# The last two gate columns of a hybrid encoder layer: two plain products, or a fourth seven-product unit

## The chip, the cores and the metric

The kernel runs on one core of a Trainium2 chip. The metric is the device time of one execution in microseconds (us), and for a kernel the median of its runs. A profile is one further execution that the hardware profiler recorded. Engines are named as the profile names them: PE is the matrix engine (PEld its weight loads), DVE the vector engine, ACT the scalar engine, POOL the GpSimd engine, SP the sync engine, which here only issues transfers. POOL issues transfers too, on a queue of its own.

## What is computed

One encoder layer over 1024 prompt frames and 32 sample frames, 1056 tokens in all. The part that matters here is the input product `z = h @ W_in`, whose last 2048 columns are the gates of the two branches:

```python
h = _rms_norm(x, g_pre_mix)
z = h @ w_in
qa, ka, va, qb, fb, ib, ob, ga, gb = jnp.split(z, SPLIT_POINTS, axis=-1)
...
mix = jax.nn.sigmoid(ga) * (ya @ w_br_a) + jax.nn.sigmoid(gb) * (yb @ w_br_b)
x = x + _rms_norm(mix @ w_out, g_post_mix)
```

`ya` comes from windowed attention, `yb` from a gated linear recurrence of eight heads. The kernel cuts the 2048 gate columns into 16 gate columns of 128, eight for `ga` and eight for `gb`, and writes for each the tanh of half the logit to memory.

## The kernel before

Activations lie transposed: 128 partitions of the model dimension by tokens, in three groups of 384, 384 and 288 tokens. `La[g]` and `Lb[g]` hold the high and low part of group g, eight slices of the model dimension each. A product of precision float32 is three matmuls: high weight by high part, high weight by low part, low weight by high part. A plain gate column takes, for each group, 8 slices times 3 matmuls.

The kernel runs in stages: attention with its input products (to about 356 us of the span), the recurrence with its input products (to about 826 us), the tail of gate columns that is the matter of this change (826 to 852 us), the branch products `ya @ w_br_a` and `yb @ w_br_b` (from 852 us, matmuls into `st` tiles from operand pages `oa` and weights `wt`), then the output product and the feed-forward part.

In the recurrence stage the input columns are computed in units of two columns by `unit_pieces`. A unit takes the first two token groups and the two columns as a 2 by 2 block product and needs seven block products in place of eight (a Winograd form of Strassen's scheme); each is a piece of 4 slices times 3 matmuls of 384 tokens. The block sums of the activations stand ready in `SX`: numbers 0, 2 and 7 are halves of `La`/`Lb`, numbers 1, 3, 4 and 6 are the sums in `TH0` to `TH3` with low parts `TL0` to `TL3`. The third group, of 288 tokens, takes four plain pieces of 12 matmuls out of `GX`. A unit's weights are made by `b_parts`: DVE forms four sums, and each of eight parts of 128 x 512 gets a cast on ACT (its high part, L1043) and a subtraction on DVE (its low part, L1044). The results stand in PSUM banks X, Y, Z and G; the evacuations e0 to e10 read them on ACT and DVE, and a gate column then has its tanh on ACT (L299) and its store on SP.

The heads' units come in order (q and f, then i and og); after heads 3 and 7 follows a unit of two gate columns. `unit_at` and `BU` list them. `b_raw` puts a unit's raw weights in the buffers `wr` (2) or `wb` (8) by turns, counted from the last unit. The recurrence's small steps (`tile_in`, `tile_out`, `group_out`) are hung on the pieces by number with `at`. What is left of head 7 after its last unit is hung on the tail.

The tail before is `u` and `v`, the last two gate columns as plain products of three blocks each, 24 matmuls a block. Since the recurrence uses the space of `La[1][0:4]` and `Lb[1][0:4]` for its gate tile, `back` reloads them from memory (`h_d`, eight transfers of 192 KB). The first three blocks run with the recurrence's steps, the last three with the preparation of the branch stage: POOL loads the operand pages (`a_load`, L1557: two of each product number, called (0,0) to (6,1) below), and `a_split` makes high and low parts of them, a cast on ACT (L1564) and a subtraction on DVE (L1565). The branch weights come through SP (`wa`, L1533) and are split at L228 and L229. The tile framework orders each engine's instructions by itself, after the program's order and its guess at durations.

Of the kernel before, what the change touches and what calls it, by code (L numbers as in the profile page):

```python
# [10 lines left out]
F32 = mybir.dt.float32  # L11
F32R = mybir.dt.float32r
# [47 lines left out]
def layer_kernel(  # L60
# [17 lines left out]
    def nm(s):  # L78
        n_names[0] += 1
        return f"{s}_{n_names[0]}"  # L80
# [67 lines left out]
    def in_cols(c):  # L148
        return rows_cols(w_in, 0, c, P, KT)
# [12 lines left out]
            plan.append(in_cols(b[1] * P if b[0] == "q" else GATES[b[1]][1]))  # L162
    plan.append(in_cols(GATES[N_A][1]))
    n_first = len(plan)
    plan += [in_cols(c) for _, c in GATES[14:]]
    n_gates = len(plan)
    plan += [rows_cols(w_out, 0, c * P, P, KT) for c in (*range(8), *range(8))]
    n_mix = len(plan)
    limit = [n_first]
# [7 lines left out]
    def load_next():  # L177
        _, kt, n = plan[len(ready)]
        if len(raws) == len(ready):
            load_raw()  # L180
        raw = raws[len(ready)]
        hi = wp.tile([P, kt, n], F32R, tag="wb", name=nm("wh"), bufs=8)
        lo = wp.tile([P, kt, n], F32R, tag="wb", name=nm("wl"), bufs=8)
        S.copy(hi[:], raw[:])
        if lo_by[0] == "vector":
            V.tensor_tensor(lo[:], raw[:], hi[:].bitcast(F32), op=ALU.subtract)
        else:
            S.mul(lo[:], raw[:], -1.0)
            gdma(lo[:], raw[:], accum_op=ALU.add)
        ready.append((hi, lo))  # L190
# [89 lines left out]
    def unit(out):  # L280

        cell = []

        def get_w():
            if not cell:
                cell.append(next_w())
            return cell[0]
        return [(get_w, g, out) for g in range(3)]
# [6 lines left out]
    def gate_out(dst):  # L295
        def out(g, b):
            o, n = GR[g]
            t = gtile()
            S.activation(t[:, :n], b[:, :n], AF.Tanh, scale=0.5)  # L299
            dma(dst[:, o:o + n], t[:, :n])  # L300
        return out
# [698 lines left out]
    def rows4(t):  # L1000
        return [t[:, k, :] for k in range(4)]
# [15 lines left out]
    for h in range(8):  # L1017
        unit_at[h] = len(BU)
        BU += [(1280 + h * P, 2304 + h * P), (3328 + h * P, 4352 + h * P)]
        if h in G_AFTER:  # L1020
            BU.append(tuple(GATES[G_AFTER[h] + a][1] for a in range(2)))
    NB = len(BU)
    raw_b, ready_b, gens_b, n_b = {}, [], {}, [0]

# [65 lines left out]
    with right("bp") as bp:  # L1090
        def bt(tag, cols, bufs, dt=F32):
            return bp.tile([P, cols], dt, tag=tag, name=nm(tag), bufs=bufs)
# [11 lines left out]
        HD = [{} for _ in range(8)]  # L1104
        ahead_b = 3

        def unit_pieces(u, f1_dest, f1, f2_dest, f2):

            c = {}

            def piece(t, seq, x, n, first):
                def run():
                    if first and t not in c:
                        c[t] = bank(pb, t, 1)
                    b_prepare(min(8 * u + seq + ahead_b, 8 * NB - 1))
                    w = ready_b[8 * u + seq]
                    o = c[t][:, :n]
                    for k in range(4):  # L1120
                        wh, wl = w[:, 0, k, :], w[:, 1, k, :]
                        E.matmul(o, wh, x[0][k], start=first and k == 0, stop=False,  # L1122
                                 skip_group_check=True)
                        E.matmul(o, wh, x[1][k], start=False, stop=False, skip_group_check=True)
                        E.matmul(o, wl, x[0][k], start=False, stop=k == 3, skip_group_check=True)
                return run

            def st(t, seq, first=False):
                return piece(t, seq, SX[seq], 384, first)

            def cl(t, seq, first=False):
                return piece(t, seq, GX[seq], 288, first)

            def b(t, n=384):
                return c[t][:, :n]

            def e0():
                c["s1c"] = bt("s1c", GMAX, 1)
                S.copy(c["s1c"][:], b("X"))

            def e2():
                c["U2"] = f1_dest()
                V.tensor_tensor(c["U2"], c["s1c"][:], b("Y"), op=ALU.subtract)

            def e5():
                c["U3"] = f2_dest(1)
                V.tensor_tensor(c["U3"], b("Y"), c["s1c"][:], op=ALU.subtract)

            def e6():
                V.tensor_tensor(c["U3"], c["U3"], b("Z"), op=ALU.subtract)  # L1150
                f2(1, c["U3"])

            def e8():
                d = f2_dest(0)
                V.tensor_tensor(d, b("Y"), c["s1c"][:], op=ALU.subtract)
                f2(0, d)

            def e10():
                V.tensor_tensor(c["U2"], c["U2"], b("Z"), op=ALU.add)
                f1(1, c["U2"])  # L1160

            def g1a():
                c["G"] = bank(pb, "G", 1)
                cl("G", 0, True)()

            def g2a():
                c["G"] = bank(pb, "G", 1)
                cl("G", 5, True)()

            return [(st("X", 0, True), e0), (g1a, None), (st("Y", 1, True), e2),  # L1170
                    (st("X", 2), lambda: f1(0, b("X"))), (cl("G", 2), lambda: f1(2, b("G", 288))),
                    (st("Y", 3), e5), (st("Z", 4, True), e6), (g2a, None), (st("Y", 6), e8),
                    (cl("G", 6), lambda: f2(2, b("G", 288))), (st("Z", 7), e10)]
# [36 lines left out]
            return unit_pieces(unit_at[h] + 1, i_dest, i_out, lambda g: bt("x0", GMAX, 1)[:], og_out)  # L1210

        def gate_unit(h):
            a, b = (gate_out(GATES[G_AFTER[h] + i][0]) for i in range(2))
            return unit_pieces(unit_at[h] + 2, lambda: gu, a,
                               lambda g: bt("x0", GMAX, 1)[:], b)

        def v_turn(h, g):
            d = HD[h]
# [183 lines left out]
        def at(m, f, *a):  # L1402
            small.setdefault(m, []).append(lambda: f(*a))
# [27 lines left out]
            for g, m in enumerate((13, 14, 16) if last else (16, 18, 21)):  # L1431
                at(m1 + m, group_out, h, g)

        def back():

            for part, t in (("La", La), ("Lb", Lb)):
                t[1][0:4] = rows4(lp.tile([P, 4, 384], F32R, tag=f"{part}10", name=nm(part)))
            for part, t in zip(h_d, (La, Lb)):
                for k in range(4):
                    dma(t[1][k].bitcast(F32), part[:, k, :])  # L1440

        def more():
            limit[0] = n_gates
            load_next()

        at(len(pieces) - 1, back)
        at(len(pieces) - 2, more)
        w_sums = [(3, 0, 0, None), (4, 0, 1, None), (1, 0, 0, None), (6, 1, 0, None),
                  (3, 0, 1, None), (4, 1, 1, None), (1, None, None, 4), (6, None, None, 1)]
        def block_sum(dst, src, acc):  # L1450
# [29 lines left out]
        for m, (run, ev) in enumerate(pieces):  # L1480
# [2 lines left out]
                ev()  # L1483
            for f in small.pop(m, ()):
                f()
        u, v = (unit(gate_out(dst)) for dst, _ in GATES[14:])
        tail = [u[0], u[2], v[0], v[2], u[1], v[1]]
        n_bank[0] += 2
        stream(tail[:3], {m - len(pieces): f for m, f in small.items()})
    bctx.close()  # L1490


# [88 lines left out]
        small[m] = [lambda x=x: both(a_prepare, x) if isinstance(x, int) else both(a_split, *x)  # L1581
                    for x in at_m]
    small[3].append(lambda: a_load(2, 1, gdma))
    stream(tail[3:], small)
    lctx.close()
    pctx.close()
    with right("mp") as mp:
# [1368 lines left out]
```

## Time and profile before

| | |
|---|---|
| median of three runs | 1937.41 us (1937.32 to 1943.33) |
| the profiled execution | 1941.95 us |
| its span, from first to last instruction | 1940.2 us |
| matmuls | 14523 |
| busy share of DVE, ACT, POOL | 76%, 53%, 20% |
| moved by DMA | 329 MB, 170 GB/s on average |

The busy shares are means over stages with different limits. In the views below, a window's row gives its start and end, its length, then the busy time of PE, PEld, DVE, ACT and POOL, each with its number of instructions, then the clock that PE was granted, the busy share of the 16 DMA engines and what they moved in GB/s. A row of the timeline gives start, duration, engine, source line, operation, tiles and shape; in square brackets stand the idle time of the engine before it and what ended that.

### The profile page before, as it was taken

To read this page: it belongs to the slowest core of one execution; us is meant where nothing else is said; L and a number is where in the kernel's file an instruction comes from. 1 tells how busy PE (TensorE), PEld (TensorE's weight loads), DVE (VectorE), ACT (ScalarE), POOL (GpSimd) and SP (SyncE) were. 2 spreads that over 40 slices of the span, in tenths; PEclk is the share of its full clock that TensorE was granted. 3 is DMA by queue.
4 is the path that set the end of the run, shared out by engine and by line. 5 is a ranking of instruction groups with operands and counts; after the bars stand their busy time and mean duration, and the time that the engine had idled before them with its cause. 6 is when DMAs were issued, how large, how long until landed. Compare 5 with 4: busy or idle time off the path is not lost.

```text
span 1940.2 us, 38175 instructions
## 1 busy us (share of the span) xinstructions
PE 1919.0 (99%) x14523; PEld 1900.5 (98%) x14523; DVE 1473.5 (76%) x3201; ACT 1028.7 (53%) x2214; POOL 383.8 (20%) x530
## 2 busy tenths in 40 slices
PE   8999999999999999999999999999999999999999
PEld 8999999999999999999999999999999999999998
DVE  6777777788887888756796878778787786768872
ACT  7667777666666666553445763333333336534432
POOL 2111211001101010022321113444644430000000
PEclk9999999999999999999999999999999999999999
DMA  8534443545537464489979784566897357754343
GB/s 267 151 106 134 120 139 84 156 111 142 146 95 155 121 139 101 127 288 308 289 194 298 242 274 126 166 168 186 165 181 190 110 179 235 221 179 155 116 132 87
DMA packets 319599, 329.11 MB, mean 170 GB/s; under 512 B 17432, under 2 KB 277435, under 8 KB 319416
## 3 DMA queue, kind: packets, MB, share of 16 engines
q1 hardware_dynamic: 274152, 218.92, 36.6%
q0 software_dynamic: 45136, 107.70, 23.1%
q8 instruction: 114, 1.87, 0.4%
q14 instruction: 69, 0.57, 0.1%
q10 hardware_dynamic: 128, 0.06, 0.0%
HBM read 234.48 MB, written 132.47 MB: 189 GB/s over the span
## 4 chain that ended last, share of the span: by engine, by line
PE 87%; DVE 5%; DMA 3%; ACT 3%; issue 2%; SPq 0%; POOL 0%; ACTq 0%; DVEq 0%; POOLq 0%
PE st L2377 7%; PE st L2376 7%; PE st L2375 7%; PE mm L207 4%; PE mm L205 4%; PE mm L206 4%; PE st L2505 4%; PE st L2507 4%; PE st L2506 4%; PE st L1667 3%; PE st L1669 3%; PE st L1671 3%; PE st L205 2%; PE st L206 2%; PE st L207 2%; PE Y L1122 2%
## 5 line engine op out<-in xcount | busy, mean ns | idle before, releaser
L2375 PE MATMUL st<-op,wt 128*128 128x264 f32 x1232 | 348.6, 283 | 1.7 <-DVE x L1921 0.8
L2377 PE MATMUL st<-op,wt 128*128 128x264 f32 x1232 | 349.8, 284 | 0.0
L2376 PE MATMUL st<-op,wt 128*128 128x264 f32 x1232 | 347.7, 282 | 0.0
L2375 PEld LDWEIGHTS st<-op,wt 128*128 128x128 f32 x1232 | 231.2, 188 | 3.1 <-issue 1.0
L2376 PEld LDWEIGHTS st<-op,wt 128*128 128x128 f32 x1232 | 231.4, 188 | 0.0
L2377 PEld LDWEIGHTS st<-op,wt 128*128 128x128 f32 x1232 | 230.8, 187 | 0.0
L2505 PE MATMUL st<-dop,wt 128*128 128x264 f32 x616 | 174.5, 284 | 1.0 <-ACT S L2520 0.7
L2507 PE MATMUL st<-dop,wt 128*128 128x264 f32 x616 | 174.3, 283 | 0.0
L2506 PE MATMUL st<-dop,wt 128*128 128x264 f32 x616 | 173.8, 283 | 0.0
L2034 ACT CAST wt<-wu 128x512 fp32r<-128x512 f32 x126 | 76.0, 618 | 176.3 <-POOL wu L2043 71.4
L205 PE MATMUL mm<-La,wh 128*128 128x384 f32 (+1 forms) x480 | 158.2, 330 | 0.0
L206 PE MATMUL mm<-Lb,wh 128*128 128x384 f32 (+1 forms) x480 | 155.4, 324 | 0.5 <-DVE Lb L784 0.4
L207 PE MATMUL mm<-La,wl 128*128 128x384 f32 (+1 forms) x480 | 155.0, 323 | 0.2 <-DVE wl L759 0.2
L2035 DVE TENSOR_TENSOR wt<-wu,wt 128x512 fp32r<-128x512 f32 x126 | 86.5, 695 | 46.0 <-ACT wt L2034 46.0
L2505 PEld LDWEIGHTS st<-dop,wt 128*128 128x128 f32 x616 | 115.6, 188 | 1.7 <-ACT S L2520 1.2
L2506 PEld LDWEIGHTS st<-dop,wt 128*128 128x128 f32 x616 | 115.6, 188 | 0.0
L2507 PEld LDWEIGHTS st<-dop,wt 128*128 128x128 f32 x616 | 115.5, 188 | 0.0
L2139 ACT CAST wt<-wd 128x512 fp32r<-128x512 f32 (+1 forms) x84 | 48.9, 586 | 90.0 <-PE st L2507 70.1
L206 PEld LDWEIGHTS mm<-Lb,wh 128*128 128x128 f32 x480 | 90.4, 189 | 1.7 <-DVE Lb L784 1.4
L207 PEld LDWEIGHTS mm<-La,wl 128*128 128x128 f32 x480 | 90.2, 188 | 0.5 <-DVE wl L759 0.5
L1043 ACT CAST wt<-wu 128x512 fp32r<-128x512 f32 x108 | 65.1, 618 | 47.8 <-DVE wu L1051 23.9
L1122 PE MATMUL G<-La,wt 128*128 128x288 f32 x288 | 90.4, 314 | 0.0
(628 smaller groups left out, 6353.9 us busy)
## 6 DMA issues: line engine op xcount, KB each, us to landing
wu<-in_w_up_dram SPq DMA_DIRECT2D x42, 512.0 KB
wu<-in_w_in_dram SPq DMA_DIRECT2D x36, 512.0 KB
w_d<-in_w_down_dram POOLq DMA_DIRECT2D x24, 704.0 KB, 8.6
a_d<-Up SPq DMA_DIRECT2D x21, 528.0 KB
wr<-in_w_in_dram SPq DMA_DIRECT2D x21, 512.0 KB
s_d<-sm SPq DMA_DIRECT2D x40, 264.0 KB
dop<-s_d SPq DMA_DIRECT2D x16, 528.0 KB
wr<-in_w_out_dram SPq DMA_DIRECT2D x16, 512.0 KB
```

The lines of the kernel that those rows point to most:

```text
L205: E.matmul(ps, wh, a, start=first and n == 0, stop=False)
L206: E.matmul(ps, wh, b, start=False, stop=False)
L207: E.matmul(ps, wl, a, start=False, stop=last and n == len(ks) - 1)
L1122: E.matmul(o, wh, x[0][k], start=first and k == 0, stop=False, skip_group_check=True)
L2034: S.copy(t[:, 0], src)
L2035: V.tensor_tensor(t[:, 1], src, t[:, 0].bitcast(F32), op=ALU.subtract)
L2375: E.matmul(o, wh, xh, start=first and k == 0, stop=False, skip_group_check=True)
L2376: E.matmul(o, wh, xl, start=False, stop=False, skip_group_check=True)
L2377: E.matmul(o, wl, xh, start=False, stop=k == 3, skip_group_check=True)
L2505: E.matmul(o, wh, xh_, start=first and k == 0, stop=False, skip_group_check=True)
L2506: E.matmul(o, wh, xl_, start=False, stop=False, skip_group_check=True)
L2507: E.matmul(o, wl, xh_, start=False, stop=k == ng - 1, skip_group_check=True)
```

## The change

The last two gate columns become one more unit, number 18 (`unit_at[8]`), with pieces in an order of their own (`last`). Its first five pieces run with the recurrence's steps, its last six with the preparation of the branch stage. The two plain columns, their weights in the plan and the reload `back` go.

```diff
     n_first = len(plan)
-    plan += [in_cols(c) for _, c in GATES[14:]]
-    n_gates = len(plan)
     plan += [rows_cols(w_out, 0, c * P, P, KT) for c in (*range(8), *range(8))]
...
+    unit_at[8] = len(BU)
+    BU.append(tuple(GATES[14 + a][1] for a in range(2)))
     NB = len(BU)
...
+            def g2x():
+                c["G"] = bank(pb, "X", 1)
+                cl("G", 5, True)()
+
+            if last:
+                return [(st("X", 0, True), e0), (st("Y", 1, True), e2), (st("Y", 3), e5),
+                        (st("Z", 4, True), e6), (st("Y", 6), e8), (st("Z", 7), e10),
+                        (st("X", 2), lambda: f1(0, b("X"))), (g1a, None),
+                        (cl("G", 2), lambda: f1(2, b("G", 288))), (g2x, None),
+                        (cl("G", 6), lambda: f2(2, b("G", 288)))]
...
-        def back():
-
-            for part, t in (("La", La), ("Lb", Lb)):
-                t[1][0:4] = rows4(lp.tile([P, 4, 384], F32R, tag=f"{part}10", name=nm(part)))
-            for part, t in zip(h_d, (La, Lb)):
-                for k in range(4):
-                    dma(t[1][k].bitcast(F32), part[:, k, :])
...
+        tail = gate_unit(8)
+        pieces += tail[:5]
...
-        u, v = (unit(gate_out(dst)) for dst, _ in GATES[14:])
-        tail = [u[0], u[2], v[0], v[2], u[1], v[1]]
-        n_bank[0] += 2
-        stream(tail[:3], {m - len(pieces): f for m, f in small.items()})
+        for m in sorted(small):
+            for f in small[m]:
+                f()
...
-    stream(tail[3:], small)
+    for m, (run, ev) in enumerate(tail[5:]):
+        run()
+        if ev is not None:
+            ev()
+        for f in small.get(m, ()):
+            f()
```

Line numbers of the kernel move by a few. Three places in the order of the instructions are spoken of later.

POOL, at the start of the tail, before: the load of the sample's recurrent state `S`, then the operand pages `oa` in the order (0,0), (1,0), (2,0), (0,1), (1,1), (2,1), (3,0), (3,1), then the first gate tiles `ta`. In brackets stand the engines and queues that a row waits for.

```order
L1321 DMA S_10813<-in_state_hgrn_dram 128x128 [waits DMASW2_49,DMASW5_49,DVE_49,PE_49]
L1557 DMA oa_10934<-ya_d 128x1056
L1557 DMA oa_10933<-sa_d_112 128x1056 [waits DMASW4_49]
L1557 DMA oa_10932<-ya_d 128x1056
L1557 DMA oa_10931<-ya_d 128x1056 [waits DMASW6_49]
L1557 DMA oa_10930<-sa_d_112 128x1056
```

The same place of POOL's order in the changed kernel.

```order
L1331 DMA S_10816<-in_state_hgrn_dram 128x128 [waits DMASW2_49,DMASW5_49,DVE_49,PE_49]
L1554 DMA oa_10938<-ya_d 128x1056 [waits PE_49]
L1554 DMA oa_10937<-sa_d_112 128x1056 [waits DMASW4_49]
L1554 DMA oa_10936<-ya_d 128x1056
L1554 DMA oa_10935<-ya_d 128x1056 [waits DMASW6_49]
L1554 DMA oa_10934<-sa_d_112 128x1056
```

The first page load now waits for PE; the count that it waits for is that of the last matmul of the tail's fifth piece, which reads `TH3`, in whose space the pages lie. All others stand behind it on POOL.

ACT, where the tail hands over to the branch stage, before: tanh of a tail gate (L299), casts of operand pages (L1564) and of branch weights (L228), and the first copy out of an `st` tile (L1675).

```order
L299 ACTIVATE gt_11019<-G_10992 128x384 [waits DMAHW7_49,PE_49,Activation_49]
L1564 CAST oa_10933<-oa_10933 128x1056 [waits DMASW4_49]
L1564 CAST oa_10932<-oa_10932 128x1056 [waits DMASW5_49]
L228 CAST wt_10989<-wa_10956 128x512
L1564 CAST oa_10931<-oa_10931 128x1056 [waits DMASW6_49]
L299 ACTIVATE gt_11059<-X_11028 128x384 [waits DMAHW3_49,PE_49,Activation_49]
L1564 CAST oa_10930<-oa_10930 128x1056 [waits DMASW7_49]
L228 CAST wt_11024<-wa_10956 128x512 [waits DMAHW0_49]
L228 CAST wt_11044<-wa_10986 128x512 [waits DMAHW1_49]
L228 CAST wt_11062<-wa_10986 128x512 [waits DMAHW2_49]
L1675 COPY as_11107<-st_11093 128x264 [waits PE_49]
```

ACT at the same place in the changed kernel.

```order
L297 ACTIVATE gt_11026<-G_10999 128x288 [waits DMAHW0_49,PE_49,Activation_49]
L1561 CAST oa_10937<-oa_10937 128x1056 [waits DMASW4_49]
L1561 CAST oa_10936<-oa_10936 128x1056 [waits DMASW5_49]
L226 CAST wt_10996<-wa_10963 128x512 [waits DMAHW1_49]
L297 ACTIVATE gt_11066<-X_11035 128x288 [waits DMAHW1_49,PE_49,Activation_49]
L1561 CAST oa_10935<-oa_10935 128x1056 [waits DMASW6_49]
L1561 CAST oa_10934<-oa_10934 128x1056 [waits DMASW7_49]
L226 CAST wt_11031<-wa_10963 128x512 [waits DMAHW2_49]
L226 CAST wt_11051<-wa_10993 128x512 [waits DMAHW2_49]
L226 CAST wt_11069<-wa_10993 128x512 [waits DMAHW3_49]
L1677 COPY as_11114<-st_11100 128x264 [waits PE_49]
```

The same eleven rows, from a tail gate's tanh to the first copy; the two tanh are of 288 tokens instead of 384, and the first of them waits for the ninth piece of the tail instead of the fifth block.

DVE, in head 0 of the recurrence, before: from the first factor products to the evacuation e2 (L1143, into `vt`) of the unit i and og.

```order
L1286 TENSOR_TENSOR d_925_5221<-d_925_5221,tf 128x384
L1287 TENSOR_TENSOR ke_5222<-ke_5222,tf 128x384
L1288 COPY dec_5202<-cb 128x3
L1291 SCALAR_TENSOR_TENSOR tq_5058<-tq_5058,cb 128x384
L1044 TENSOR_TENSOR wt_5240<-sa_5115,wt_5240 128x512
L1143 TENSOR_TENSOR vt_5259<-s1c_5200,Y_5239 128x384
```

DVE in the changed kernel, some 15 rows earlier, up to the scans (L1245).

```order
L1044 TENSOR_TENSOR wt_5185<-sa_5115,wt_5185 128x512
L1155 TENSOR_TENSOR tf<-Y_5017,s1c_4998 128x384
L1056 TENSOR_TENSOR wu_5021<-wu_5021 128x512
L1044 TENSOR_TENSOR wt_5240<-sa_5115,wt_5240 128x512
L1159 TENSOR_TENSOR x_907_5037<-x_907_5037,Z_5096 128x384
L1245 SCALAR_TENSOR_TENSOR cb<-resets,cb 128x384 x2
```

With one more unit, the raw weights of units 0 and 1 change buffers; the subtraction for part `wt_5240` now stands ahead of the scans and no longer directly ahead of e2.

More of the change, by code (lines that the diff above doesn't have):

```diff
@@ L1105, in layer_kernel, with unit_pieces @@
         ahead_b = 3
-        def unit_pieces(u, f1_dest, f1, f2_dest, f2):
+        def unit_pieces(u, f1_dest, f1, f2_dest, f2, last=False):
             c = {}
@@ L1212, in gate_unit @@
         def gate_unit(h):
-            a, b = (gate_out(GATES[G_AFTER[h] + i][0]) for i in range(2))
-            return unit_pieces(unit_at[h] + 2, lambda: gu, a,
-                               lambda g: bt("x0", GMAX, 1)[:], b)
+            a, b = (gate_out(GATES[G_AFTER[h] + i if h < 8 else 14 + i][0]) for i in range(2))
+            return unit_pieces(unit_at[h] + 2 * (h < 8), lambda: gu, a,
+                               lambda g: bt("x0", GMAX, 1)[:], b, h == 8)
         def v_turn(h, g):
@@ L1432, in layer_kernel @@
                 at(m1 + m, group_out, h, g)
-        def back():
-            for part, t in (("La", La), ("Lb", Lb)):
-                t[1][0:4] = rows4(lp.tile([P, 4, 384], F32R, tag=f"{part}10", name=nm(part)))
-            for part, t in zip(h_d, (La, Lb)):
-                for k in range(4):
[L1440 to L1447, printed above, removed]
+        tail = gate_unit(8)
+        pieces += tail[:5]
         w_sums = [(3, 0, 0, None), (4, 0, 1, None), (1, 0, 0, None), (6, 1, 0, None),
```

## The prediction

> **What bounds the kernel now.** First the page's head, engine shares and chain.
>
> ```profile
> span 1940.2 us, 38175 instructions
> PE 1919.0 (99%) x14523; PEld 1900.5 (98%) x14523; DVE 1473.5 (76%) x3201; ACT 1028.7 (53%) x2214; POOL 383.8 (20%) x530
> PE 87%; DVE 5%; DMA 3%; ACT 3%; issue 2%; SPq 0%; POOL 0%; ACTq 0%; DVEq 0%; POOLq 0%
> ```
>
> PE is busy almost always, so a matmul that goes should be worth its spacing, unless another engine or a transfer then ends last at that place. Next the windows around the places that the change touches.
>
> ```profile
> 380.00:400.00 20.00, 18.93 (x122) 18.62 (x121) 20.00 (x51) 14.58 (x34) 1.15 (x3) 1.00 0.05 5
> 800.00:820.00 20.00, 20.00 (x137) 19.78 (x136) 11.74 (x27) 8.36 (x23) 2.63 (x5) 1.00 0.53 136
> 820.00:840.00 20.00, 20.00 (x140) 19.96 (x138) 8.34 (x41) 8.76 (x32) 3.18 (x6) 1.00 0.68 244
> 840.00:860.00 20.00, 19.72 (x139) 19.51 (x138) 11.52 (x16) 11.46 (x18) 6.00 (x12) 1.00 0.84 258
> 860.00:880.00 20.00, 17.38 (x142) 16.98 (x141) 15.32 (x23) 13.21 (x20) 6.03 (x10) 1.00 0.99 327
> ```
>
> The tail (826 to 852) has no PE idle at all. The branch stage's start loses 2.9 us of PE (0.28 and 2.62), with DMA at 0.99: there the stage is bound by transfers, not by PE. In head 0 of the recurrence DVE is full and PE loses 1.07 us. Now the PE rows of the tail, and its three waits behind it.
>
> ```profile
> 826.06 0.47 PE L205 MATMUL G<-La,wh 128*128 128x384 f32 x1
> 839.97 0.38 PE L205 MATMUL Z<-La,wh 128*128 128x288 f32 x1
> 843.25 0.34 PE L205 MATMUL G<-La,wh 128*128 128x384 f32 x1
> 851.57 0.28 PE L1667 MATMUL st<-oa,wt 128*128 128x264 f32 x1
> 855.16 0.39 PE L1667 MATMUL st<-oa,wt 128*128 128x264 f32 x1 [0.28 <-ACT as L1675]
> 864.33 0.39 PE L1667 MATMUL st<-oa,wt 128*128 128x264 f32 x1 [0.41 <-ACT as L1675]
> 869.72 0.36 PE L1667 MATMUL st<-oa,wt 128*128 128x264 f32 x1 [2.21 <-DVE R L1679]
> ```
>
> **The matmuls.** The last two blocks, 48 matmuls of 384 tokens, take 843.25 to 851.57, 8.32 us or 173 ns each; the 24 of 288 before them 3.28 us, 137 ns each. The tail before is 4 blocks of 24 of 384 (96) and 2 of 24 of 288 (48). After, it is 7 pieces of 12 (84) and 4 of 12 (48). So 12 matmuls of 384 go: 12 x 0.173 = **-2.1 us**.
>
> **What hides the unit's extra vector work.** DVE gets 8 subtractions at 0.68 (as at 386.81 below), 4 sums at as much and 5 evacuations at 0.55 (as at 387.42), 10.9 us, and loses two subtractions of 128 x 1024, about 2.7 by the same rate: some 8 us more between 800 and 842. The windows 800 to 840 have DVE busy for 20.1 of 40 us and ACT for 17.1; PE reads the parts in order, so I cost this at nothing. If that cover failed, PE would wait for each part.
>
> **One new wait inside the tail.** Head 7 ends in a chain: last recurrence matmul, copy, square, twelve small DVE steps, scaling on ACT, transposes on PE.
>
> ```profile
> 833.32 0.49 PE L1387 MATMUL tr<-ident,vk 128*128 128x128 f32 x3
> 833.52 0.26 ACT L1367 COPY z<-so 32x128 f32<-32x128 f32 x1 [1.99 <-PE so L1366]
> 837.14 0.69 ACT L1379 ACTIVATE vk<-vk,rs 128x128 f32<-128x128 f32 x2 [1.29 <-DVE rs L222]
> 837.74 0.39 ACT L1379 ACTIVATE z<-z,rs 32x128 f32<-32x128 f32 x1
> 839.73 0.38 PE L1387 MATMUL tr<-ident,vk 128*128 128x128 f32 x2
> ```
>
> From the recurrence matmul's end (the transposes at 833.32 follow it) to the last scaled tile (837.74 + 0.39) it takes 4.8 us, and PE has 6.4 us of blocks meanwhile. After, PE has only 23 matmuls of 384 and three transposes there, 4.2 us, and DVE squeezes one evacuation (0.55) into the chain. Bounds: 0, if the order absorbs it, to 1.2, the shortage of 0.6 plus that evacuation; I take **+0.7**, nearer the upper end, as the order puts that evacuation between the twelve steps. Behind the waiting transposes stands the rest of piece six.
>
> **Head 0.** There DVE holds PE up.
>
> ```profile
> 379.56 2.45 DVE L1235 TENSOR_TENSOR_SCAN cb<-resets,cb 128x384 f32<-128x384 bf16 x3 [1.44 <-ACT cb L1233]
> 386.81 0.68 DVE L1044 TENSOR_TENSOR wt<-sa,wt 128x512 fp32r<-128x512 f32 x1
> 387.42 0.55 DVE L1143 TENSOR_TENSOR vt<-s1c,Y 128x384 f32<-128x384 f32 x1
> 388.02 0.44 PE L1122 MATMUL Y<-TH,wt 128*128 128x384 f32 x1 [1.07 <-DVE vt L1143]
> ```
>
> The subtraction at 386.81 now stands ahead of the scans, where DVE idles 1.44 us. That frees 0.61 (start to start) ahead of the evacuation that PE waits for; but it and its cast also stand ahead of the rows that lead to the scans. Bounds 0 and -0.61; I take **-0.4**, nearer the row.
>
> **The hand-over.** Before, five page loads went out at the tail's start:
>
> ```profile
> 826.65 0.54 POOL L1557 DMA_DIRECT2D oa<-ya_d  x1
> 849.09 1.61 POOL L1627 DMA_DIRECT2D ta<-ta_d  x3 [0.35 <-issue]
> DMA to landing us min/median/max: 4.2/6.1/11.8
> oa<-ya_d POOLq DMA_DIRECT2D x4, 528.0 KB, 6.8
> 828.00:840.00 12.00, 12.00 (x85) 11.96 (x83) 3.42 (x18) 4.17 (x16) 1.28 (x3) 1.00 1.01 369
> 840.00:852.00 12.00, 12.00 (x78) 12.00 (x77) 6.05 (x8) 7.00 (x11) 3.19 (x6) 1.00 0.72 210
> ```
>
> After, the first waits on POOL for the fifth piece, which ends near 839, with the others and the gate tiles `ta` queued behind it. The loads come 12 us later: 5 x 0.54 = 2.7 MB move from a stretch at 369 GB/s into one that already carries 210 x 12 = 2.5 MB. The dropped reload (8 x 0.19 MB) frees only the earlier stretch, and PE did not wait for it at 843.25, so it is worth nothing on the path. From 839 to 852 DMA can move 13 x 0.369 = 4.8 MB and is asked for 5.2: a backlog of 0.4 MB, **1.1 us** at that rate, when the branch stage's own transfers begin.
>
> Does PE wait for the pages? ACT works through them in order.
>
> ```profile
> 847.66 0.49 ACT L299 ACTIVATE gt<-G 128x384 f32<-128x384 f32 x1 [2.79 <-PE G L207]
> 848.05 2.04 ACT L1564 CAST oa<-oa 128x1056 fp32r<-128x1056 f32 x2
> 852.21 1.07 ACT L1564 CAST oa<-oa 128x1056 fp32r<-128x1056 f32 x1
> 853.17 1.66 ACT L228 CAST wt<-wa 128x512 fp32r<-128x512 f32 x3
> 854.73 0.38 ACT L1675 COPY as<-st 128x264 f32<-128x264 f32 x1
> ```
>
> This run of eleven rows starts when the fifth block ends and is nearly unbroken to 855.11, where PE waits for the copy (855.16): ACT sets the time here, not PE. The changed kernel has the same eleven rows (two tanh shorter by 0.08 each). It starts when the ninth piece ends. PE's tail, 2.1 shorter and 0.7 held up, ends 1.4 earlier, at 850.2; the ninth piece 24 x 0.137 = 3.3 before, at 846.9, against 847.41. So the copy ends 0.5 + 0.1 = 0.6 us earlier, not 1.4: ACT takes **+0.8** back. The fifth page must land by about 851.5; sent out at 841, that is 10.5 us, between the rows' median and maximum.
>
> Then the wait at 869.72. It hangs on branch weights:
>
> ```profile
> 867.89 1.14 ACT L228 CAST wt<-wa 128x512 fp32r<-128x512 f32 x2 [3.61 <-DMA wa<-in_w_br_a_dram]
> ```
>
> With DMA full from 852 on, this landing moves with the backlog rather than with PE. Bounds: 0 (issued 0.6 earlier, landing 0.6 earlier) to +1.7 (0.6 lost, 1.1 later); I take **+0.8**, near the middle, as the rows of both kinds are as near.
>
> Sum: -2.1 + 0.7 - 0.4 + 0.8 + 0.8 = **-0.2 us**. Behind 870 the order is that of before. The profiled execution took 1941.95 us, 1.75 around its span; -0.2 gives 1941.75. The runs' median lies 4.54 lower: 1937.41 - 0.2 = **1937.2 us**.
>
> [...] The tail's tanh use two buffers, so each waits for the store two before it. Before, one waited long:
>
> ```profile
> 828.27 1.70 SPq L1440 DMA_DIRECT2D Lb<-h_d  x3
> 831.55 0.32 SPq L300 DMA_DIRECT2D tb_d<-gt  x1
> 841.29 0.49 ACT L299 ACTIVATE gt<-Y 128x384 f32<-128x384 f32 x1 [3.16 <-DMA tb_d<-gt]
> ```
>
> The store issued at 831.55 had landed only by 841.29, 9.7 us later, with page loads on POOL's queue and three reloads ahead of it on SP's own. [...]
>
> **The rivals.** (1) The gain stays: pages land in time and the weights follow PE. The ACT run and the DMA wait then take nothing: -2.1 + 0.7 - 0.4 = -1.8, or -2.7 with the two best bounds: 1934.7 to 1935.6. For it: PE is 99% busy. Against: ACT ended last at 855.16, DMA at 869.72. 0.2. (2) Slower: a gate store is late amid the page loads. The tanh that opens the ACT run (846.9) needs the store issued near 842.7 (the sixth piece ends near 841.6, then an evacuation of 0.55 and a tanh of 0.49); from a latency of 4.2 us on, each further us delays the run and PE. At the 9.7 seen it costs 5.5: -0.6 + 5.5 = +4.9, or +2.3 if PE's later waits of 0.41 and 2.21 vanish into it: 1939.7 to 1942.3. For it: 2.7 MB on one queue in the same us. Against: no reload ahead of the stores. 0.25. That the change leaves the products as they were is out: the order holds 12 matmuls fewer.
>
> **How the numbers follow.** The forecast, 0.55, spans 1935.5 to 1939.0 by its bounds (-1.9 and +1.6: each term at its lower and its upper bound, ACT's fixed). The range takes in both rivals: 1934.4 to 1942.6. Within 0.3% (about what a measurement of this kernel can tell) means 1931.6 to 1943.2. No sum reaches the lower end: 0.03, for a cause not seen. The upper needs a latency beyond the 9.7, or more than one late store: 0.07. The rest, 0.90, is no measurable change.
>
> **What would show it.** PE 14511 matmuls; the first `st` matmul at 849.5 to 850.5; the first page load near 839; an idle of 0 to 1.2 us before transposes near 839; the first copy ending 854 to 855.5; PE's wait near 869 grown to 2.5 to 4 us; head 0's wait 0.4 to 1.1. Wrong would be: tanh waiting for stores over 1 us (second rival), or `st` running unbroken to 870 (first rival).

## The result, and the profile after

The changed kernel took 1944.05 us (median of nine runs, 1942.08 to 1946.55), the kernel before 1937.32 us beside it (nine runs, 1936.85 to 1943.33). The change costs 6.7 us by the medians; the ratio taken over all runs is 1.0032, with a 95% interval of 1.0024 to 1.0041, or 4.6 to 7.9 us. The forecast was 1937.2 and the range ended at 1942.6. The profiled execution took 1944.05 us, the median itself. That of before had taken 1941.95, 4.6 above its median.

Head, engine shares and chain of the page after:

```profile
span 1942.3 us, 38173 instructions
PE 1921.0 (99%) x14511; PEld 1901.1 (98%) x14511; DVE 1481.1 (76%) x3216; ACT 1030.7 (53%) x2221; POOL 381.2 (20%) x530
PE 85%; DVE 7%; DMA 3%; ACT 3%; issue 2%; SPq 0%; POOL 0%; ACTq 0%; DVEq 0%; POOLq 0%
```

Twelve matmuls fewer, and PE is busy 2.0 us longer: some matmuls must run slower. The windows after say where; their columns are those of the windows before.

```profile
380.00:400.00 20.00, 19.84 (x125) 19.28 (x123) 20.00 (x53) 13.79 (x33) 1.61 (x3) 1.00 0.36 107
820.00:840.00 20.00, 20.00 (x126) 19.17 (x126) 12.87 (x49) 10.46 (x32) 2.85 (x6) 1.00 0.24 73
840.00:860.00 20.00, 16.94 (x107) 16.06 (x106) 11.05 (x14) 10.05 (x16) 4.50 (x9) 0.87 1.05 378
860.00:880.00 20.00, 19.44 (x154) 19.23 (x153) 14.88 (x21) 13.69 (x21) 7.81 (x14) 0.96 0.98 319
```

DMA falls from 244 GB/s to 73 between 820 and 840 and rises from 258 to 378 between 840 and 860, with a busy share above 1 (a packet counts whole in the window in which it starts). In that second window PE loses 3 us, and its granted clock is 0.87. PE's rows there:

```profile
851.11 0.39 PE L1671 MATMUL st<-oa,wt 128*128 128x264 f32 x1 [0.56 <-DVE oa L1562]
...
854.07 0.39 PE L1669 MATMUL st<-oa,wt 128*128 128x264 f32 x1 [1.36 <-ACT wt L226]
...
855.69 0.59 PE L1669 MATMUL st<-oa,wt 128*128 128x264 f32 x1 [1.11 <-ACT as L1677]
856.07 0.42 PE L1671 MATMUL st<-oa,wt 128*128 128x264 f32 x1
856.29 0.42 PE L1673 MATMUL st<-oa,wt 128*128 128x264 f32 x1
...
861.78 0.28 PE L1673 MATMUL st<-oa,wt 128*128 128x264 f32 x1
861.90 0.28 PE L1669 MATMUL st<-oa,wt 128*128 128x264 f32 x1
...
864.21 0.39 PE L1669 MATMUL st<-oa,wt 128*128 128x264 f32 x1 [0.56 <-ACT as L1677]
```

Three waits follow each other: for the low half of a page, for a weight cast, for the first copy. Behind them the matmuls start 0.22 us apart (856.07 to 856.29); from 861.78 on it is 0.12 again. The clock record has 0.50 from 854.92 for 6.83 us. The page's clock line cannot show this: its tenths read 9 throughout. ACT's rows, where those waits come from:

```profile
844.96 0.49 ACT L297 ACTIVATE gt<-X 128x384 f32<-128x384 f32 x1 [2.53 <-DMA tb_d<-gt]
...
848.39 0.41 ACT L297 ACTIVATE gt<-G 128x288 f32<-128x288 f32 x1 [1.98 <-DMA tb_d<-gt]
...
854.74 0.62 ACT L226 CAST wt<-wa 128x512 fp32r<-128x512 f32 x1 [0.20 <-DMA wa<-in_w_br_a_dram]
855.26 0.37 ACT L1677 COPY as<-st 128x264 f32<-128x264 f32 x1
861.76 0.62 ACT L226 CAST wt<-wa 128x512 fp32r<-128x512 f32 x1 [6.13 <-DMA wa<-in_w_br_a_dram]
...
863.78 0.37 ACT L1677 COPY as<-st 128x264 f32<-128x264 f32 x1
```

Two tanh wait for gate stores (the second rival's sign), then a cast waits 6.13 us for branch weights with the second copy behind it. POOL's rows, with the idle time ahead of them:

```profile
837.70 0.54 POOL L1554 DMA_DIRECT2D oa<-ya_d  x1 [12.51 <-PE tr L1397]
...
847.07 0.53 POOL L1554 DMA_DIRECT2D oa<-sa_d  x1 [6.22 <-DMA yb_d<-sg]
849.13 0.54 POOL L1629 DMA_DIRECT2D ta<-ta_d  x1 [1.53 <-PE X L1125]
```

The page loads come at 837.70, when the fifth piece ends, as foreseen (this execution is some 2 us ahead of the one that the working used). Not foreseen: page (3,0) waits for a store of recurrence rows that shares its space, and the gate tiles `ta` wait for the unit's very last piece, which reads the 288-token operand in whose space they lie. In the kernel before, that operand's last reader was the third block from the end. Its rows, from its second trace (e1 below):

```profile
843.79 1.05 POOL L1557 DMA_DIRECT2D oa<-sa_d  x2 [5.91 <-DVE oa L1565]
845.19 1.60 POOL L1627 DMA_DIRECT2D ta<-ta_d  x3 [0.36 <-issue]
```

POOL waits nearly as long there for page (3,0), but for other work, and both loads go out 4.5 and 3.1 us ahead of the branch stage's first matmul (848.29). In the changed kernel page (3,0) goes out 1.7 us ahead of it (848.80), and `ta` 0.3 us behind it.

Two more rows show the recurrence, PE's waits in head 0 and in a later head:

```profile
385.11 0.44 PE L1122 MATMUL Y<-TH,wt 128*128 128x384 f32 x1 [0.17 <-DVE vt L1143]
...
620.05 0.52 PE L1312 MATMUL tr<-ident,ke 128*128 128x128 f32 x3 [0.74 <-DVE dec L1298]
```

The wait of 1.07 has shrunk to 0.17; one of 0.74 is new, at a place the prediction didn't look at.

### The profile page after: what moved, and what is told of

Read it like the earlier page. It is cut to its first block, busy times and chain, and to the rows that moved or that the text cites. A ratio compares the mean times of both kernels' runs of the same rounds, so it can differ in the third digit from the quotient of the medians.

```text
span 1942.3 us, 38173 instructions
## 1 busy us (share of the span) xinstructions
PE 1921.0 (99%) x14511; PEld 1901.1 (98%) x14511; DVE 1481.1 (76%) x3216; ACT 1030.7 (53%) x2221; POOL 381.2 (20%) x530
## 4 chain that ended last, share of the span: by engine, by line
PE 85%; DVE 7%; DMA 3%; ACT 3%; issue 2%; SPq 0%; POOL 0%; ACTq 0%; DVEq 0%; POOLq 0%
PE st L2379 7%; PE st L2378 7%; PE st L2377 7%; PE mm L203 5%; PE mm L205 5%; PE mm L204 5%; PE st L2507 4%; PE st L2509 4%; PE st L2508 4%; PE st L1673 3%; PE st L1671 3%; PE st L1669 3%; PE st L203 2%; PE st L204 2%; PE st L205 2%
```

## The experiments

The theory: every transfer of the hand-over got late at once, and taking one away exposes the next. Its rivals: a single late transfer is to blame (gate stores, pages, `ta`, weights), the halved clock is the cost itself, ACT's order is wrong, or the swapped raw buffers are it. Ratios are against the kernel before, run beside each kernel on the same chip.

**e1: the kernel before again.** Nothing edited.

> The kernel before, unchanged, for a second trace of it. The profiled execution of before took 1941.95 us, 4.6 over its median of 1937.32, and the trace of after says that 2.0 of it are two waits in the first 63 us (0.50 at 53.20, 0.97 at 62.65) that after does not show. If these are chance, this trace lacks them and spans about 1936; if they belong to before, it shows them again. The wait of 2.21 us at 869.72 should be there in both cases, with the granted clock at 1.00.

It took 1935.38 us, and its only PE wait between 838 and 872 is this:

```profile
851.88 0.39 PE L1667 MATMUL st<-oa,wt 128*128 128x264 f32 x1 [0.28 <-ACT as L1675]
```

The wait of 2.21 at 869.72, on which the DMA term of the prediction rested, is not in it: one of two executions of the same kernel has it. The first was also slower early on: to PE's 2500th matmul, in code that all kernels share, it took 377.2 us, this one 374.4 and the changed kernel 375.2. Against e1 the changed kernel's 8.7 us stand as follows, by PE's start times: +0.8 to that matmul, +0.8 in the recurrence (429.1 for 428.2, to PE's 5350th matmul, in head 7), -1.1 from there to the first `st` matmul, called the tail here (44.6 for 45.7), +6.8 in the 640 matmuls of the branch stage that follow its first (84.9 for 78.2), +1.4 in all the rest. All of the 6.8 is lost in the first 70 of the 640; from there on the two traces run in step.

This compares two single executions, and e1 is 1.9 us below the median of before (2.8 below that of its own rounds, 1938.22). Against the first trace (81.2) the 640 matmuls took only 3.7 us more. The medians, 6.7 apart, less the tail and the recurrence leave about 7 for the rest, an estimate that is nearer to e1.

That stretch of 640, 78.1 us at 0.122 each, is what the experiments compare. "Half clock" is the length of the record at 0.50.

| run | median us | ratio, 95% interval | 640 matmuls | PE idle in it | half clock |
|---|---|---|---|---|---|
| before, profiled first | 1937.32 | | 81.2 | 2.9 | 0 |
| e1 (one execution) | 1935.38 | | 78.2 | 0.3 | 0 |
| changed kernel | 1944.05 | 1.0032, 1.0024 to 1.0041 | 84.9 | 3.6 | 6.8 |
| e2 | 1944.39 | 1.0033, 1.0021 to 1.0044 | 85.1 | 4.3 | 6.8 |
| e3 (660) | 1945.87 | 1.0042, 1.0028 to 1.0056 | 88.4 | 5.0 | 6.8 |
| e4 | 1943.95 | 1.0031, 1.0019 to 1.0042 | 84.4 | 4.8 | 3.4 |
| e5 | 1946.06 | 1.0049, 1.0035 to 1.0063 | 85.6 | 5.8 | 6.8 |
| e6 | 1943.42 | 1.0034, 1.0021 to 1.0046 | 85.1 | 4.9 | 3.4 |
| e7, of before | 1946.75 | 1.0053, 1.0040 to 1.0066 | 84.2 | 4.3 | 3.4 |
| e8 | 1942.68 | 1.0029, 1.0018 to 1.0041 | 84.7 | 3.2 (2.4 more ahead of it) | 6.8 |
| e9 | 1940.90 | 1.0017, 1.0008 to 1.0026 | 83.7 | 2.8 | 6.8 |
| e10 | 1943.58 | 1.0028, 1.0017 to 1.0039 | 84.2 | 3.2 | 6.8 |
| e11 | 1939.19 | 1.0004, 0.9995 to 1.0013 | 81.8 | 2.2 | 3.4 |
| e12, of before | 1940.92 | 1.0014, 1.0005 to 1.0022 | 82.9 | 3.0 | 3.4 |
| e13 | 1948.49 | 1.0055, 1.0042 to 1.0068 | 90.8 | 11.3 | 10.2 |
| e14 | 1941.24 | 1.0015, 1.0006 to 1.0023 | 84.2 | 3.9 | 6.8 |
| e15, of before | 1945.02 | 1.0035, 1.0021 to 1.0048 | 84.6 | 4.3 | 6.8 |
| e16 (692) | 1945.37 | 1.0044, 1.0031 to 1.0056 | 86.3 | 1.9 | 0 |
| e17 (649) | 1938.89 | 1.0006, 0.9997 to 1.0015 | 80.8 | 1.4 | 0 |

Medians that lie within 2 us of each other are not told apart here; the last three columns are of one execution each.

**e2: no gate store can hold a tanh.** The last unit's first four gate buffers lie in the space that the dropped reload freed.

```diff
+                    t = lp.tile([P, 4, GMAX], F32, tag="La10", name=nm("gt"))
+                    four.extend([1] + [t[:, k] for k in range(4)])
```

> After, with four buffers of its own for the first four tanh of the last unit (the space of La10, free by then), so that no tanh there waits for a gate store. Theory S (stores): the tanh at 844.96 and 848.39 waited 2.53 and 1.98 us for stores, the run of casts behind them opened late, PE lost 3.0 us before 855.7 and then ran at half the clock for 6.8 us, which cost 3.0 more. It expects the copy `as` near 853, PE's waits before it under 1.2 us in sum, a clock of 1.00, and 1938 to 1940.5 us. Theory P (pages): pages land every 1.7 us from 841.96 to 850.56 and would hold the casts in any case. It expects the copy at 854.5 or later and 1942 to 1944.

ACT's rows:

```profile
842.04 0.49 ACT L297 ACTIVATE gt<-X 128x384 f32<-128x384 f32 x1
...
845.23 0.41 ACT L297 ACTIVATE gt<-G 128x288 f32<-128x288 f32 x1 [1.74 <-PE G L1125]
...
854.28 0.62 ACT L226 CAST wt<-wa 128x512 fp32r<-128x512 f32 x1 [2.47 <-DMA wa<-in_w_br_a_dram]
854.81 0.37 ACT L1687 COPY as<-st 128x264 f32<-128x264 f32 x1
```

Both waits for stores are gone, ACT is 3 us ahead, and loses it to the branch weights: the copy starts at 854.81 where it was 855.26, and PE waits 3.38 us for it. The time is the same. The second rival's sign was there, but the stores alone are not the cause.

**e4, e5, e9: pages early, gate tiles early, both.** In e4 the last unit's four sum pieces multiply the plain operand in place of the sums (so that the last two gate columns are not computed), which frees the pages' space 12 us sooner. In e5 the pieces of 288 tokens go ahead of the last two of 384, which frees that of `ta`. e9 is both.

```diff
-                return piece(t, seq, SX[seq], 384, first)
+                return piece(t, seq, SX[0 if last and seq in (1, 3, 4, 6) else seq], 384, first)
...
-                        (st("Z", 4, True), e6), (st("Y", 6), e8), (st("Z", 7), e10),
-                        (st("X", 2), lambda: f1(0, b("X"))), (g1a, None),
+                        (st("Z", 4, True), e6), (st("Y", 6), e8), (g1a, None),
                         (cl("G", 2), lambda: f1(2, b("G", 288))), (g2x, None),
-                        (cl("G", 6), lambda: f2(2, b("G", 288)))]
+                        (cl("G", 6), lambda: f2(2, b("G", 288))), (st("Z", 7), e10),
+                        (st("X", 2), lambda: f1(0, b("X")))]
```

> After, with the four pieces of the last unit that read operand sums reading the plain operand instead (that part of the result is not computed), so that the page loads need not wait for the fifth piece. All else, the two gate buffers and the dropped reload too, stays. If the late pages are at the root of all (they delay stores, casts and weights), the loads go out near 826, no tanh waits over 1 us for a store behind them, the clock stays at 1.00, and the time is 1934.5 to 1937. If the stores are late for another reason, the waits of 2 us before the tanh stay and the time is above 1940.

> After, with the four 288-token pieces of the last unit's second half ahead of its two 384-token pieces (before, the 288-token blocks also stood ahead of the last 384-token ones). Theory G (gate tiles): the loads of the gate tiles `ta` wait on POOL for the last matmul that reads the 288-token operand, because they take its space; in after that is the last piece of all (849.13), in before the middle of the tail (845.19 in the second trace, 3 us ahead of the branch stage). The page loads queued behind them, and with them the branch weights on the other queue, come late, PE stalls 3 to 4 us in one wait and the clock halves. G expects `ta` issued 3 to 4 us ahead of the first `st` matmul, the long wait under 1.5 us, and 1938 to 1940. If the late pages or stores alone did it: 1942 to 1944.

> e4 and e5 together: the last unit's sum pieces read the plain operand (that part is not computed), so pages load early, and its 288-token pieces stand ahead of its last two. e4 had early pages but gate tiles `ta` held to 849.2 by the last piece; e5 had the order but `ta` held to 847.9 behind a page load that waited for a row store delayed among the pages. Theory G2: either alone is enough to push `ta`, two pages and the branch weights into the same few us, so each experiment alone showed no gain. It expects `ta` issued by 846, a wait for weights under 1.5 us instead of 3.84, no clock drop or a single one, and 1937 to 1939.5. If order and pages do not matter: 1943 to 1946.

With early pages (825.5 to 827.6 in e4) `ta` is still issued at 849.18 and a weight cast waits 6.71 us. In e5 `ta` stands on POOL behind page (3,0), which waits 6.6 us for the store, and gets out only 1.2 us sooner. Neither gains alone. Both together gain: `ta` is issued at 845.42, and the ratio is 1.0017 for 1.0032, about half of the loss.

**e7, e12: the kernel before, made late.** In e7 its two blocks of 288 tokens come last, so that `ta` is late. In e12 a copy on POOL holds the page loads back to 833.8.

```diff
-        tail = [u[0], u[2], v[0], v[2], u[1], v[1]]
+        tail = [u[0], v[0], u[1], v[1], u[2], v[2]]
...
+    held = lp.tile([P, 1], F32, tag="held", name="held")
+    G.tensor_copy(held[:], outs_g[-2][:, 0:1])
```

> The kernel before, with its tail's two 288-token blocks moved from the third and fourth place to the last two. Nothing of the new unit is in it. Theory G expects `ta` to wait for the end of the tail here too, a PE wait of 2 us or more near 853 to 860, and 1940 to 1943. If G is wrong the time stays at 1937 to 1938.5.

> The kernel before, with a copy of one column on POOL ahead of the first five page loads that reads the tail's second tanh (near 833 in the second trace), so that the loads start 10 us later and the tail is otherwise as before. If late pages alone bring the stall, whatever the unit does: a wait of 2 us or more between 850 and 870 and 1939 to 1943. If the cover of the tail is what counts and 17 us suffice: 1936.5 to 1938.

Late pages alone cost the kernel before 2.7 us (a ratio of 1.0014, 1.0005 to 1.0022), with all its 12 matmuls in place. e7 cost more, but its reload is needed earlier too and PE waits 2.4 us for it near 837: it doesn't isolate `ta`.

**e6: the raw buffers as before.** The last unit takes `wb` out of turn, so that all others keep theirs.

```diff
-            odd = (NB - u) % 2
+            odd = (NB - 1 - u) % 2 if u < NB - 1 else 1
```

> After, with units 0 to 17 taking their raw weights through the same buffers as before (after swapped the two kinds for all of them, as their choice counts from the last unit); the last unit keeps the eight-buffer kind. Theory B (buffers): from head 4 on after loses 1.6 to 2 us against before (a wait of 0.74 at 620 in all four traces of after, and a slow drift), because weights come later through the other kind. It expects no wait over 0.3 at 620, head 0's wait back at 0.6 to 1.1, and 1942 to 1943, 1 to 2 us below after. If the swap is harmless, 1943.5 to 1944.5 and the wait at 620 stays.

The wait at 620 is gone, head 0's is 0.59, as in e1, and the recurrence takes 428.0 in place of 429.1 us. The traces agree on it: 429.1 to 429.2 in all nine with the swapped buffers, 428.0 to 428.1 in the five with e6's, 428.2 to 428.7 in the five of the kernel before and its variants. The median, 0.6 lower, can't show it.

**e10: the third weights in space of their own**, that of the dropped reload again.

```diff
-        if k > 3 and k % 3 == 2:
+        if k == 2:
+            t = spare_l()[:, 0:KT * P].rearrange("p (k c) -> p k c", c=P)
+        elif k > 3 and k % 3 == 2:
```

> After, with the third pair of raw branch weights in a space of its own (La10, free by then), so that it loads before the tail and the fourth pair's load waits for the split of the first pair (near 843) instead of the second (near 855). Theory W (weights): the wait of ACT for the fourth pair (6.13 us in after, 6.71 in e4, 3.56 in e5, 6.14 in e6, 6.27 in e7) is what PE's longest stall hangs on, and late gate tiles and pages only slow that load. It expects that wait under 1 us, PE's wait at 857 to 866 gone; the waits of 1.36 and 1.11 near 855 (theory S, stores) and one half-clock window may stay: 1939 to 1942. If the load's own start is not what counts: 1943 to 1945.

ACT's rows of the third pair's casts and, behind them, of the fourth pair's first, which had waited 6.13 us:

```profile
854.40 1.14 ACT L226 CAST wt<-sp 128x512 fp32r<-128x512 f32 x2
855.44 0.62 ACT L226 CAST wt<-wa 128x512 fp32r<-128x512 f32 x1
```

No wait is left at them, nor PE's behind them at 864. But the three waits ahead stay (0.57, 1.36, 1.24), and with them 6.8 us of half clock, and the median is lower by only 0.5.

**e3, e16: PE kept busy while it waits.** Matmuls that nobody reads: 20 ahead of the first unit's third operand in e3, and in e16 also 32 ahead of the second unit's.

```diff
+                for r in range(fill.pop(0) if fill else 0):
+                    if r == 0:
+                        jt = tr_bank()
+                    E.matmul(jt[:, 0:H], first_w[0][:, 0, 0], opa[0, 0, 0][:, 0, 0], start=True,
+                             stop=True, skip_group_check=True)
...
+        fill, first_w = [0, 0, 20, 0, 0, 32], []
```

> After, with 20 matmuls of 264 columns into a bank that nobody reads, put where PE waits for the copy `as` (1.36 and 1.11 us of idle). No wait is shortened. Theory C (clock): the idle of 3.0 us in 5.4 is what drops the granted clock to one half from 854.9 to 861.7, and that costs 3.0 us. It expects a clock of 1.00 throughout and 1940.5 to 1942, as PE's later waits for weights take some of the 3.0 back. If the clock is not what costs, the time stays at 1943.5 to 1944.5.

> The changed kernel, with products that nobody reads (20 ahead of the first unit's third operand, 32 ahead of the second unit's third) in the two places where e3_fill_the_wait and the changed kernel left TensorE idle between 850 and 870 us. If the half clock is a cost of its own: granted clock 1.00 from 825 to 900 us, waits of the weights and operands as late as before, and a median of 1942 to 1943.5 us, 2 to 3.4 below e3 (1945.87). If only the lateness of the transfers counts, the half clock running beside work that waits anyway: 1945.5 to 1946.5, as e3.

In e3 the clock holds through the first waits (1.00 from 849 to 862), PE reaches the next copy early and waits 3.94 us for it at 864.93; the drop comes there (0.62 from 862 to 870). In e16 it is 1.00 through the whole branch stage, and the median is that of e3 (1945.37 and 1945.87). PE's filler rows and then ACT's rows tell why:

```profile
852.75 2.45 PE L1670 MATMUL tr<-oa,wt 128*128 128x264 f32 x19
861.16 4.04 PE L1670 MATMUL tr<-oa,wt 128*128 128x264 f32 x32
```

```profile
862.35 0.62 ACT L226 CAST wt<-wa 128x512 fp32r<-128x512 f32 x1 [5.70 <-DMA wa<-in_w_br_a_dram]
...
864.37 0.37 ACT L1683 COPY as<-st 128x264 f32<-128x264 f32 x1
```

At full clock PE is ready for the second unit's third operand at 861.16, and the copy that it needs ends at 864.74: the weights landed at 862.35. In the changed kernel they landed at 861.76 and the copy ended at 864.15, with PE 0.56 us early at half clock. So there the halved clock ran inside a wait that would have ended no sooner. e10 took that wait away and left the half clock: each covers the other. The fillers are not free, though: the 32 end 0.3 us after that copy (865.04), and 1.5 us of idle time stay at 856.70, so e16 can't exclude a gain of less than a microsecond.

**e13, e15: ACT's order.** The weight casts go ahead of the pages (0,1) and (1,1), in the changed kernel and in the kernel before.

```diff
-    for m, at_m in enumerate(((0, 1, (0, 0), (1, 0)), ((2, 0), 2), ((0, 1),), ((1, 1), 3), (4,), (5,))):
+    for m, at_m in enumerate(((0, 1, (0, 0), (1, 0)), ((2, 0), 2), (3,), (4,), (5,), ((0, 1), (1, 1)))):
```

> After, with ACT's order at the hand-over changed alone: the casts of the fourth, fifth and sixth branch weights ahead of those of two pages that PE needs 48 matmuls later. Theory O (order): in after PE's waits of 1.36 and 1.11 near 855 hang on a run of ACT in which 2.04 us of page casts stand ahead of the weights, and the next raw weights load only when these are split. O expects the copy `as` near 853.5, the two waits under 0.8 in sum, the weights' load about 2 us earlier, and 1940 to 1942.5. If the stores and the landings decide, not the order: 1943 to 1945.

> The kernel before with e13's order alone, to see whether the order would help it as much. Its second trace has 0.28 us of idle at the hand-over and no clock drop, its first 2.90; O expects nothing to gain but the chance of the longer wait: 1936 to 1938.5, within 1 us of before.

ACT's rows in e13:

```profile
854.23 0.62 ACT L226 CAST wt<-wa 128x512 fp32r<-128x512 f32 x1 [3.55 <-DMA wa<-wa_d]
859.34 0.62 ACT L226 CAST wt<-wa 128x512 fp32r<-128x512 f32 x1 [4.49 <-DMA wa<-in_w_br_a_dram]
```

Worse in both kernels: in e13 the casts themselves wait for transfers, with the tanh and two pages behind them, and PE waits 10.92 us at 862.53. In e14, below, the same order makes e11 worse too (1.0015 for 1.0004; PE waits 3.94 us at 853.75). The order that the theory asked for is no remedy; no other was tried.

**e8, e11, e14, e17: several at once.** e8 is e5's order, e6's buffers and the operand sums laid out in reverse, so that the first page finds its space free some 7 us sooner (830.15) and the sixth 1.5. e11 adds e10's space and a third gate buffer there; e14 adds e13's order to e11; e17 adds nine matmuls that nobody reads to e11, where its PE waited.

```diff
+            t = spare_l()[:, KT * P:KT * P + GMAX] if n_own[0] % 3 == 1 else gtile()
...
+    for j in range(3, -1, -1):
+        TH.insert(0, tp.tile([P, 4, 384], F32R, name=f"TH{j}"))
+        TL.insert(0, tp.tile([P, 4, 384], F32R, name=f"TL{j}"))
```

> After, with e5's order and e6's buffers, and the operand sums laid out in reverse in memory, so that each of the first five page loads waits for a piece two to eight us earlier than the fifth. If theories G and B hold and the late pages cost the rest, the hand-over stalls under 1 us and the gain of the unit is left: 1934.5 to 1936.5, 1 to 3 us under before. If the late pages cost nothing, as e4 says, it is e5 and e6 in sum: 1937 to 1938.5.

> After, with e10's space, a third gate buffer beside it, e5's order, e6's buffers and the reversed sum operands of e8. If S, W, G2 and B name all that the change lost at the hand-over and in the recurrence, PE waits under 1.5 us in sum from 825 to 880, the clock stays at 1.00, and the time is 1934 to 1936.5, at or under before. If the transfers as a whole (13 us of full DMA) are the limit, a wait of 2 us or more remains somewhere and the time is 1938 to 1941.

> e11 with e13's order. In e11 PE still waits 1.13 at 850.86 for a weight cast and 1.06 at 852.43 for its DVE half, and the clock halves for one window of 3.4 us (1.7 us lost). O expects all three gone: idle under 0.6 from 825 to 880, clock 1.00, and 1935 to 1937, 1 to 3 us under before in the same rounds. If the full DMA decides, the wait moves to the next weights and the time stays at 1938.5 to 1940.

> e11_four_together, with nine products that nobody reads ahead of the second unit's first operand, where its TensorE waited 1.13 us for the weight cast. If the half clock is a cost of its own: granted clock 1.00, idle time under 1.1 us between 849 and 870, and 1936.5 to 1938.0 us, at or just below the kernel before (ratio 0.999 to 1.000). If not: as e11, 1939 to 1940 us.

e8 is not told apart from the changed kernel: its tanh wait 5.35 and 2.36 us for stores, two buffers being too few. e11, with the stores and the weights taken care of too, takes 1939.19 us, 1.0004 of before. PE's waits in it, between 838 and 872:

```profile
850.86 0.39 PE L1683 MATMUL st<-oa,wt 128*128 128x264 f32 x1 [1.13 <-ACT wt L226]
...
852.43 0.39 PE L1687 MATMUL st<-oa,wt 128*128 128x264 f32 x1 [1.06 <-DVE wt L227]
```

Neither of them hangs on a transfer directly; what is left is ACT's and DVE's work on pages and weights. e17 kept the clock, and its stretch less nine fillers (1.1 us) is 79.7 for 81.8, but its median, 0.3 lower, doesn't show that, nor its ratio (1.0006 for 1.0004). No version here is faster than the kernel before.

## Why the prediction was wrong, step by step

**The matmuls, -2.1, and the wait before the transposes, +0.7: right in their sum, by luck.** The tail took 44.6 us for 45.7, and 44.2 to 44.6 in the other runs with its pieces in the change's order: -1.1 to -1.5, where the two terms make -1.4. But the transposes came at 837.38, only some 0.15 us late. And the matmuls of 384 tokens took 24.5 us for e1's 25.9, 1.4 less and not 2.1: at some of the places where PE changes from one tile or operand to another, the next matmul started 0.24 to 0.31 us later, not 0.173, at 14 in the new order for 7 in the old. The extra vector work cost nothing that PE shows.

**Head 0, -0.4: right there, wrong as a term.** Against e1 its wait fell from 0.59 to 0.17. But the swap of raw buffers touches every head's unit, and 0.74 appeared at 620.05. The recurrence came out 0.8 us longer than in e1 and 1.1 longer than in e6: a term of about +1, where one place had been priced.

**The ACT run, +0.8, and the DMA wait, +0.8: the step that failed.** In place of 1.6 us the branch stage's start took 6.8 more than in e1. By PE's start times 3.3 of it stand behind the first copy (855.69), where the ACT run had been priced, and 6.8 behind the second (864.21), whose weights landed late. The cause named was right, page loads moved into a stretch that was full already: DMA's share is above 1 from 840 to 860, and e12 shows 2.7 us for late pages alone. Three things in the working were wrong. First, the backlog was charged once, to the weights, as 1.1 us of bytes. In truth much on the two queues got late together: a store shares space with page (3,0), `ta` lies behind the unit's last piece, the gate buffers are two. The order in which space came free set when each was issued, and the prediction read POOL's order only to the fifth page. Those issued between 836 and 860 were also longer under way: page loads took 6.8 (`sa_d`) and 7.6 us (`ya_d`) to land, by their medians, for 5.8 and 6.8 between 826 and 852 in before. Second, the rival of the late gate store was priced as a delay that ends with the store, and doubted because no reload would stand ahead of it; behind three reloads a store took 2.2 us in e12 (last section). It came true (2.53 and 1.98 us), yet e2 shows that without it the weights end last at nearly the same time. Third, the working was made against one execution that held 2.9 us of idle time there; e1 held 0.3, so in it there was hardly any wait into which a new delay could vanish.

**Not in any term: the clock.** After its waits PE's clock is 0.50 for 6.83 us; the 27 matmuls in it cost 0.098 us more each, 2.65 us. By PE's own count this is the second part of the 6.8, after 3.3 us more idle time than in e1. The remaining 0.8 are the edges of three more waits: a matmul lasts 0.28 us where the next would start after 0.12, and the first one behind a wait takes 0.1 longer (854.07 to 854.29). But e16 shows that the half clock is hardly a price by itself in the changed kernel: without it PE waits for the weights instead.

**The rival "the gain stays": wrong.** e11 says what it would have taken: with five things changed together (the operand sums' order, the pieces' order, the raw buffers, a third gate buffer, space for the third weights) the time came back to that of before, with nothing left over. Its stretch of 640 still takes 81.8 us for e1's 78.2. Which of the five could be left out, no run shows.

**Open.** The 1.4 us more than in e1 behind the 640 matmuls is no cost of the change that could be told: in an order that is the same for all, the rest took 1006.6 to 1010.8 us over the nineteen traces, 1007.2 in e1 and 1008.6 in the changed kernel, and e14 and e17 are below e1. Whether e11 without any half clock would win a microsecond the medians can't tell. Nor was it tried to free the pages' space as early as in before without losing the sums.

## What to carry to other kernels

Where a stage hands over to one that starts with loads, count what the old stage's last pieces still hold: each operand's last reader sets when the space, and with it the transfer, comes free, and a piece that saves matmuls but reads more operands to the end moves all those dates (here `ta` went out 0.3 us behind the branch stage's first matmul, not 3.1 ahead of it). When several transfers get late into one full stretch, as here, removing the wait that the profile names may only show the next one (e2 took away the stores' waits of 2.53 and 1.98 us, and PE waited 3.38 for a copy behind the weights); price them together, and test them together. Profile the kernel before twice before a term is built on a wait of 2 us.

## What the runs showed of the hardware

PE's clock was halved behind waits at the hand-over, and not by the length of a wait alone. In the changed kernel the waits of 1.36 and 1.11 us (854.07 and 855.69) go with 6.83 us at 0.50, and in e10 waits of 1.36 and 1.24 with 6.8. In e6 nearly the same waits as in the changed kernel (1.38 and 1.11) go with 3.4. A single wait of 1.8 us in e12 goes with 3.4, one of 2.21 in before with none, and the waits of 1.50 in e16 and 1.06 in e17 with none either. In e13 a wait of 10.92 us goes with 10.2. What decides beside the length, no run tests by itself.

The gate stores of the changed kernel, issued at 838.66 and near 841.4, freed their buffers at 844.96 and 848.39:

```profile
838.66 0.32 SPq L298 DMA_DIRECT2D tb_d<-gt  x1
...
841.43 4.37 SPq L298 DMA_DIRECT2D tb_d<-gt  x2
```

That is 6.3 and 7.0 us with no reload ahead of them on SP's queue, against 9.7 with three. e12 has the case that the prediction lacked: there the store issued at 828.94 stood behind the same three reloads, but the page loads had not begun, and by the completion counts in its trace it had landed by 831.10, 2.2 us later; no tanh there waits for a store from 838 on, where one waited 3.16 us up to 841.29 in before. So beside page loads the stores took 6.3 and 7.0 us, behind reloads without page loads 2.2, and with both 9.7. The prediction's argument against the second rival, that no reload would stand ahead of the stores, falls with that.
